# ConvFFN weight sums: base transfers issued by GpSimd, history copies on ScalarE, raw weight buffers parted

## The chip, the cores and the metric

One NeuronCore of a Trainium2 chip runs the whole program in one launch. The metric is device time in microseconds (us) for one execution; the median of a few runs is given. The engines are TensorE (PE, with its weight loads shown as PEld), VectorE (DVE), ScalarE (ACT), GpSimd (POOL) and SyncE (SP). SP only issues DMAs here. POOL issues DMAs too, and it does a few small copies.

## The reference, cut to what matters

The model is a two-layer decoder trunk in fp32. Layer 0 has a convolution and window-attention mixer, layer 1 a Mamba-2 mixer, and each layer ends with a gated feed-forward block with a short causal convolution. The change touches only these two blocks:

```python
def conv_ffn(h, hist, w_gate, w_up, conv_w, conv_b, w_down):
    gate = h @ w_gate
    padded = jnp.concatenate([hist, gate], axis=1)
    gc = causal_dwconv(padded, conv_w, conv_b)            # width 3
    y = (jax.nn.silu(gc) * (h @ w_up)) @ w_down
    return y, padded[:, -(FFN_CONV_WIDTH - 1):]
```

It runs on 512 prompt tokens (history zero) and 8 samples of 8 tokens, each with its own history of 2 gate rows. All 576 tokens sit side by side in the free dimension. D_MODEL is 1024, D_FF is 2816, which is 22 tiles of 128 channels.

## The kernel before, in words

**Numbers.** Every fp32 operand of a matmul is split into a rounded high part (`AF.Copy` on ACT, type fp32r) and a remainder (subtraction on DVE), and a product is three matmuls: high by high, high by low, low by high. The helper `split` of the class `Strassen` does this for weights at L83 (ACT) and L84 (DVE).

**Pairs.** After the first four gate tiles and two up tiles, the gate and up projections are computed for two output tiles at a time, by seven block products instead of eight (a Winograd form of Strassen's scheme). One such pair is a `Strassen` object around a `Gate` or `Up` job, and 19 pairs run in each feed-forward block. The activations' sums and differences (`hq`: B11, B21, T1 to T4, B22) are made once per block. The weights' sums are made per pair, and by DMA: `load` (from L62) brings the upper rows of both tiles into a raw buffer (`self.up`, 1024 columns). It also fills four tiles `st0` to `st3` of 512 columns: each gets a base from HBM by a plain DMA of SP (L69), and then a second DMA, issued by POOL, adds to it while it writes (L70, `accum_op=ADD`). The chain of a pair is s1 = A22 + A21, then s2 = A11 + s1, then s4 = A12 + s2; s3 = A11 + A21 stands alone. A last load (`self.low`, into a second raw buffer) brings A22 by itself; `sums` splits it into `dh` and `dl`.

**Where the splits go.** `alpha` splits the raw upper rows (products p1, p2), `beta` splits s1 and s2 (p5, p6), `gamma` splits s4 and s3 (p3, p7, run in the next pair's turn), and `dh`, `dl` serve p4. When a product is done, `c11`, `c12`, `c22`, `c21` of the job combine it into a gate buffer or into the up product.

**Gate buffers.** `gate_open` takes a buffer `gbuf` of 594 columns, clears its first two columns and copies the samples' histories into it (L572, L573, both POOL). `gate_done` copies the new histories out (L580, L581, POOL), runs the convolution over it (L584 on ACT, L586 twice on DVE) and the SiLU (L589, L590 on ACT).

**Down projection between the pairs.** When four gate-up products are complete, `down` or `down7` makes the work of their part of the down projection as a generator, and the loop over pairs advances it by one step after most products (`some(1)`). `down7` is again a seven-product form; its weights come as raw tiles `[128,1024]`, and its sums are made on DVE (L830 to L836). It asks for the tile after next at the end of `sums(m)`.

**Buffers and order.** Raw weights of all kinds (`weights_load`, L283) use one tag `wr` with three buffers. The tiles `st`, `gbuf`, `gconv` and many others come from one list of 67 slots (`S`, `free`): a new tile takes the slot that was given back longest ago, and its first write waits until the former tile's last reader is done. The program is written in one order in Python; a planner then fixes the order of each engine's instructions from its own estimate of durations, and within an engine and its queue that order is kept. So an instruction that waits on SP, POOL, ACT or DVE holds all that stands behind it there.

Of the kernel before, what the change touches and what calls it, by code (L numbers as in the profile page):

```python
# [8 lines left out]
F32 = mybir.dt.float32  # L9
F32R = mybir.dt.float32r  # L10
AF = mybir.ActivationFunctionType
# [3 lines left out]
P = 128  # L15
# [37 lines left out]
class Strassen:  # L53
# [3 lines left out]
    def __init__(self, b, job, n):  # L57
        self.b, self.nc, self.job = b, b.nc, job
        s = b.sr
        self.r, self.e, self.a = s[0][:, HALF[0]], s[1][:, HALF[0]], s[1][:, HALF[1]]  # L60

    def load(self):  # L62
        b = self.b
        up, low = self.job.src
        self.up = b.weights_load(up, 1024)
        s1, s2, s3, s4 = self.s = [b.S(f"st{i}", 512) for i in range(4)]
        for s, first, more in ((s1, low[:, 512:1024], low[:, 0:512]), (s2, up[:, 0:512], s1), (s4, up[:, 512:1024], s2),
                               (s3, up[:, 0:512], low[:, 0:512])):
            self.nc.sync.dma_start(s, first)  # L69
            self.nc.gpsimd.dma_start(s, more, accum_op=ADD)  # L70
        self.low = b.weights_load(low[:, 512:1024], 512)
        self.alpha()

    def sums(self, between=None):
        b = self.b
        if between:
            between()
        self.d = b.S("dh", 512, F32R), b.S("dl", 512, F32R)
        self.split(self.low[:, 0:512], *self.d)

    def split(self, src, hi, lo):
        nc = self.nc
# [76 lines left out]
class Builder:  # L159
# [3 lines left out]
    def __init__(self, nc, tc, d, stack):  # L163
        self.nc, self.tc, self.d = nc, tc, d
        self.const = stack.enter_context(tc.tile_pool(name="const", bufs=1))
        self.xp = stack.enter_context(tc.tile_pool(name="xp", bufs=1))
        self.wp = stack.enter_context(tc.tile_pool(name="wp", bufs=1))
        self.sp = stack.enter_context(tc.tile_pool(name="sp", bufs=1))
        self.pp = stack.enter_context(tc.tile_pool(name="pp", bufs=1, space=bass.MemoryType.PSUM))
        self.dp = stack.enter_context(tc.tile_pool(name="dp", bufs=1, space=bass.MemoryType.DRAM))  # L170
        self.rings = {"mm": [0, 1, 2, 3], "aux": [4, 5, 6, 7]}
        self.idle = list(range(self.NSLOT))
        self.used = {}
        self.small = None
        self.held = {}
# [103 lines left out]
        self.warm = self.const.tile([P, 1], F32, name="warm")  # L279
        nc.scalar.activation(self.warm, self.eps, AF.Sqrt)  # L280

    def weights_load(self, src, n):
        raw = self.wp.tile([P, 1024], F32, tag="wr", bufs=3, name="wr")  # L283
        srcs = src if isinstance(src, list) else [src]
        for i, s in enumerate(srcs):
            self.nc.sync.dma_start(raw[:, i * n // len(srcs):(i + 1) * n // len(srcs)], s)
        return raw
# [271 lines left out]
    def ffn(self, l, next_norm):  # L559
        nc, d = self.nc, self.d  # L560
        self.rings = {"mm": [0, 1, 2, 3, 4, 5], "aux": [6, 7]}
        hist = so = self.S("fhist", NF * 16)
        nc.sync.dma_start(hist, d["ffn_hist"][l])
        po = self.Z("fpo", NF * 2, bufs=1)
# [3 lines left out]
        samples = lambda g: g[:, 514:594].rearrange("p (b c) -> p b c", c=10)  # L568

        def gate_open(f):  # L570
            g = gbuf[f] = self.S("gbuf", 594)
            nc.gpsimd.memset(g[:, 0:2], 0.0)  # L572
            nc.gpsimd.tensor_copy(samples(g)[:, :, 0:2], hist[:, f * 16:f * 16 + 16].rearrange("p (b c) -> p b c", c=2))  # L573
            return g

        def gate_done(f):

            g = gbuf.pop(f)
            gs = samples(g)
            nc.gpsimd.tensor_copy(so[:, f * 16:f * 16 + 16].rearrange("p (b c) -> p b c", c=2), gs[:, :, 8:10])  # L580
            nc.gpsimd.tensor_copy(po[:, f * 2:f * 2 + 2], g[:, 512:514])  # L581
            cv = self.S("gconv", 594)
            w = lambda k: self.pv(f"fw{l}", f * 3 + k)
            nc.scalar.activation(cv[:, :592], g[:, 0:592], AF.Copy, scale=w(0))  # L584
            for k in (1, 2):
                nc.vector.scalar_tensor_tensor(cv[:, :592], g[:, k:592 + k], w(k), cv[:, :592], op0=MUL, op1=ADD)  # L586
            sl = sl_of[f] = self.S("gsilu")
            b = self.pv(f"fb{l}", f)
            nc.scalar.activation(sl[:, :NP], cv[:, :NP], AF.Silu, bias=b)  # L589
            nc.scalar.activation(bt(sl[:, NP:]), cv[:, 514:594].rearrange("p (b c) -> p b c", c=10)[:, :, 0:8],  # L590
                                 AF.Silu, bias=b)
            self.free(g, cv)
# [28 lines left out]
        def waiting(p):  # L621
            a, b = PARTS[p]
            if p - 1 in SEVEN:
                for f in range(a, (a + b) // 2):
                    operands(p, f)
            return a, b

        def lead_gate(f, later=False):
            def go(half, p):
                if half == 0:  # L630
                    nc.scalar.activation(gate_open(f)[:, 2:290], p[:, :HB], AF.Copy)
                    return
                g = gbuf[f]
                nc.scalar.activation(g[:, 290:514], p[:, 0:224], AF.Copy)
                nc.scalar.activation(samples(g)[:, :, 2:10], bt(p[:, 224:288]), AF.Copy)
                if not later:
                    gate_done(f)
            return go
# [29 lines left out]
        class Gate:  # L668
# [3 lines left out]
            def c11(me, u, v):  # L672
                nc.vector.tensor_tensor(gate_open(me.f)[:, 2:290], u, v, op=ADD)
# [7 lines left out]
            def c22(me, u, v):  # L681
                g = gate_open(me.f + 1)
                nc.vector.scalar_tensor_tensor(g[:, 290:514], u[:, 0:224], -1.0, v[:, 0:224], op0=MUL, op1=SUB)
                nc.vector.scalar_tensor_tensor(samples(g)[:, :, 2:10], bt(u[:, 224:HB]), -1.0, bt(v[:, 224:HB]), op0=MUL, op1=SUB)
# [42 lines left out]
        lead(0, g23, other)  # L727
        sums = self.combine()
        next(sums)
        lead(1, g01)  # L730
        u0 = [(self.whole(d["w_up"][l, 0]), lead_up(0))]
        next(sums)
        lead(1, g23[:1])
        u1 = [(self.whole(d["w_up"][l, 1]), lead_up(1))]
# [44 lines left out]
        def down7(p):  # L779
# [47 lines left out]
            def sums(m):  # L827
                a11, a12, a21, a22 = [raw[m][:, i * n:i * n + n] for i in range(4)]
                s12, s43 = s[m, 2], s[m, 3] = self.S("sd", 2 * n), self.S("sd", 2 * n)
                nc.vector.tensor_tensor(s12[:, 0:n], a21, a22, op=ADD)  # L830
                nc.vector.tensor_tensor(s12[:, n:2 * n], s12[:, 0:n], a11, op=ADD)
                nc.vector.tensor_tensor(s43[:, n:2 * n], a11, a21, op=ADD)
                nc.vector.tensor_tensor(s43[:, 0:n], a12, s12[:, n:2 * n], op=ADD)
                d = last[m] = self.S("dd", 2 * n, F32R)
                nc.scalar.activation(d[:, 0:n], a22, AF.Copy)
                nc.vector.tensor_tensor(d[:, n:2 * n], a22, d[:, 0:n].bitcast(F32), op=SUB)  # L836
                load(m + 2)

            def fourth(m):
# [3 lines left out]
                self.free(d)  # L843

            load(0)
            split(0, 1)
            quarters_of("T1")

            def go():
                sums(0)  # L850
                yield
                quarters_of("B22")
# [43 lines left out]
            todo += [Gate(f), Up(f - 2)]  # L896
        todo.append(Up(NF - 2))
        self.sr = [self.S("st"), self.S("st")]
        tiles = iter(())
        ready = 0  # L900

        def some(n):
            for _ in range(n):
                next(tiles, None)

        prev = None
        for n, job in enumerate(todo + [None]):
# [38 lines left out]
                ready += 1  # L946
            prev = new
        some(16)
        nc.sync.dma_start(d["ffn_s"][l], so)
        nc.sync.dma_start(d["ffn_p"][l], po)  # L950
        self.free(hist, self.sr, list(self.hq.values()))
# [2 lines left out]
        a, b = waiting(len(PARTS) - 1)  # L954
# [479 lines left out]
    def mix1(self):  # L1434
# [146 lines left out]
        def ssd(g):  # L1581
# [208 lines left out]
            for t in range(4):  # L1790
                if t == 0:
                    load(0)
                if t == 0:
                    ea2 = carried(0, False)
                pair = []
                for hh in range(2):
                    pair.append(decays(2 * t + hh))
                    yield
                last = outputs(t, ea2, pair)
                if t < 3:  # L1800
                    ea2 = carried(t + 1)
                if t == 2:
                    self.free(H)
                    H.clear()
                yield
                if t % 2:
                    turn(t // 2)
                    yield from finish(t // 2, last)
                    if t == 1:
                        load(1)  # L1810
                else:
                    begin(t // 2)
# [280 lines left out]
```

## Time and profile before

| | |
|---|---|
| median of 3 runs | 1507.55 us (1506.25 to 1511.75) |
| profiled execution, device time | 1503.02 us |
| its span, first to last instruction | 1501.2 us |
| PE, DVE, ACT, POOL busy | 1450.3, 1220.6, 856.4, 319.0 us |
| DMA, SP's queue (q1) | 185.87 MB |
| DMA, POOL's queue (q0) | 39.86 MB |

The profiled execution is one of the fast ones: its device time lies 4.5 us below the median of the three. A row of the waits has the engine, the tile and line that waited, what ended the wait, the total in us, the number of times and the longest. A row of the timeline has start, duration, engine, line, operation, tiles, and in brackets the idle time of the engine before it. The first feed-forward block's pairs run from about 262 to 560 us of the span, the second's from about 1085 to 1440 us.

### The profile page before, as it was taken

The page shows a single profiled execution, that of the slowest core. Times are in us where ns is not written, and L with a number is a line of the kernel's source. Part 1 is how long each engine was busy: PE and PEld are TensorE (multiplying, and loading weights), DVE is VectorE, ACT ScalarE, POOL GpSimd, SP SyncE. Part 2 cuts the span into 40 slices and gives each one's busy share as a digit, 9 for nine tenths or more (in the row PEclk, how much of TensorE's full clock was granted, in tenths as well). Part 3 has the DMA queues.
Part 4 walks back from the last instruction along what each step waited for, and adds up shares of the span by engine and source line. Part 5 has one row for each costly group of instructions (what it writes and reads, how often), then busy time and mean ns, then how long its engine had stood idle before and what let it go on. Part 6 is the DMA issues. An engine that isn't in the chain of part 4 may idle for free. (4 is left out here: it accounts for less than half of the span.)

```text
span 1501.2 us, 29480 instructions
## 1 busy us (share of the span) xinstructions
PE 1450.3 (97%) x11035; PEld 1376.0 (92%) x11035; DVE 1220.6 (81%) x2445; ACT 856.4 (57%) x1771; POOL 319.0 (21%) x517
## 2 busy tenths in 40 slices
PE   8999999999999989999999999999999999999999
PEld 7967799998999989998998997998999999999999
DVE  7968899698888856779798778677998889898673
ACT  6357467564655533487784664566457656464450
POOL 0026202322323220011203202112022232232210
PEclk9999999999999999999999999999999999999999
DMA  7504634867787773136245245245367877777831
GB/s 224 163 29 117 176 103 120 214 173 174 184 201 198 175 185 97 57 106 187 93 141 159 97 128 172 86 130 165 121 172 186 218 179 193 182 188 198 200 108 63
DMA packets 120925, 227.60 MB, mean 152 GB/s; under 512 B 25534, under 2 KB 32702, under 8 KB 120782
## 3 DMA queue, kind: packets, MB, share of 16 engines
q1 hardware_dynamic: 98894, 185.87, 38.9%
q0 software_dynamic: 21888, 39.86, 16.1%
q8 instruction: 86, 1.41, 0.4%
q14 instruction: 57, 0.47, 0.1%
HBM read 190.54 MB, written 15.21 MB: 137 GB/s over the span
## 5 line engine op out<-in xcount | busy, mean ns | idle before, releaser
L326 PE MATMUL mm<-hh,wh 128*128 128x288 f32 x864 | 262.5, 305 | 6.6 <-ACT wh L297 5.5
L329 PE MATMUL mm<-hl,wh 128*128 128x288 f32 x864 | 259.3, 301 | 0.3 <-DVE hl L968 0.2
L330 PE MATMUL mm<-hh,wl 128*128 128x288 f32 x864 | 258.4, 300 | 0.7 <-DVE wl L298 0.7
L326 PEld LDWEIGHTS mm<-hh,wh 128*128 128x128 f32 x864 | 164.4, 191 | 15.0 <-ACT wh L297 5.7
L330 PEld LDWEIGHTS mm<-hh,wl 128*128 128x128 f32 x864 | 164.2, 190 | 4.0 <-issue 1.8
L329 PEld LDWEIGHTS mm<-hl,wh 128*128 128x128 f32 x864 | 164.1, 190 | 3.4 <-issue 1.4
L297 ACT ACTIVATE wh<-wr 128x1024 fp32r<-128x1024 f32 (+1 forms) x97 | 101.6, 1048 | 99.7 <-PE mm L329 67.5
L298 DVE TENSOR_TENSOR wl<-wr,wh 128x1024 fp32r<-128x1024 f32 (+1 forms) x97 | 121.0, 1251 | 32.8 <-ACT wh L297 32.2
L83 ACT ACTIVATE wh<-st 128x512 fp32r<-128x512 f32 x152 | 91.0, 623 | 61.8 <-DMA st<-st 21.2
L70 POOL DMA_DIRECT2D st<-st x76 | 66.8, 885 | 272.1 <-DMA st<-st 53.3
L510 DVE TENSOR_TENSOR x<-x,mm 128x288 f32<-128x288 f32 x192 | 85.1, 449 | 43.4 <-PE mm L330 42.7
L326 PE MATMUL mm<-yh,wh 128*128 128x288 f32 x384 | 115.3, 301 | 0.2 <-DVE x L510 0.2
L330 PE MATMUL mm<-yh,wl 128*128 128x288 f32 x384 | 114.7, 299 | 0.0
L329 PE MATMUL mm<-yl,wh 128*128 128x288 f32 x384 | 114.1, 298 | 0.0
L84 DVE TENSOR_TENSOR wl<-st,wh 128x512 fp32r<-128x512 f32 x152 | 101.4, 684 | 13.0 <-ACT wh L83 12.9
L114 PE MATMUL x<-hqT,wh 128*128 128x288 f32 x304 | 90.6, 298 | 0.0
L117 PE MATMUL x<-hqT,wh 128*128 128x288 f32 x304 | 90.4, 297 | 0.0
L118 PE MATMUL x<-hqT,wl 128*128 128x288 f32 x304 | 90.1, 296 | 0.0
L586 DVE SCALAR_TENSOR_TENSOR gconv<-gbuf,par,gconv 128x592 f32<-128x592 f32 x88 | 72.9, 830 | 9.1 <-ACT gconv L584 8.4
L326 PEld LDWEIGHTS mm<-yh,wh 128*128 128x128 f32 x384 | 72.3, 188 | 3.5 <-issue 1.8
L330 PEld LDWEIGHTS mm<-yh,wl 128*128 128x128 f32 x384 | 72.3, 188 | 1.0 <-issue 0.4
L329 PEld LDWEIGHTS mm<-yl,wh 128*128 128x128 f32 x384 | 72.3, 188 | 0.5 <-issue 0.2
(462 smaller groups left out, 4830.3 us busy)
## 6 DMA issues: line engine op xcount, KB each, us to landing
st<-in_w_up SPq DMA_DIRECT2D x80, 256.0 KB, 5.1
wr<-in_w_down SPq DMA_DIRECT2D x80, 256.0 KB, 3.3
wr<-in_w_in_o SPq DMA_DIRECT2D x40, 512.0 KB, 3.6
st<-st POOLq DMA_DIRECT2D x76, 256.0 KB, 4.4
st<-in_w_gate SPq DMA_DIRECT2D x72, 256.0 KB, 3.1
wr<-in_w_gate SPq DMA_DIRECT2D x26, 512.0 KB, 4.1
wr<-in_w_up SPq DMA_DIRECT2D x24, 512.0 KB, 5.0
st<-in_w_up POOLq DMA_DIRECT2D x40, 256.0 KB, 5.8
```

The source lines that it names most:

```text
L83: nc.scalar.activation(hi, src, AF.Copy)
L84: nc.vector.tensor_tensor(lo, src, hi.bitcast(F32), op=SUB)
L114: m = nc.tensor.matmul(out, hi[:, ws], xh, start=first and k == 0, stop=False, skip_group_check=skip)
L117: nc.tensor.matmul(out, hi[:, ws], xl, start=False, stop=False, skip_group_check=skip)
L118: nc.tensor.matmul(out, lo[:, ws], xh, start=False, stop=k == 3, skip_group_check=skip)
L297: nc.scalar.activation(hi[:, a:b], raw[:, a:b], AF.Copy)
L298: nc.vector.tensor_tensor(lo[:, a:b], raw[:, a:b], hi[:, a:b].bitcast(F32), op=SUB)
L326: first = nc.tensor.matmul(out, hi[:, ws], xh[:, sl], start=i == 0, stop=False)
L329: nc.tensor.matmul(out, hi[:, ws], xl[:, sl], start=False, stop=False)
L330: nc.tensor.matmul(out, lo[:, ws], xh[:, sl], start=False, stop=i == n - 1)
L510: nc.vector.tensor_tensor(self.x[m][:, sl], self.x[m][:, sl], p[:, :HB], op=ADD)
L586: nc.vector.scalar_tensor_tensor(cv[:, :592], g[:, k:592 + k], w(k), cv[:, :592], op0=MUL, op1=ADD)
```

## The change

- The bases of the four sums are issued by POOL (`nc.gpsimd.dma_start`) in the order s1, s3, s2, s4, all four ahead of the four accumulating DMAs, which now come in the same order. SP no longer issues them.
- `self.low` leaves the raw buffers: it goes into a slot of the list `S` (tile `a22`), which is given back once it is split.
- The clearing of two columns in `gate_open` goes from POOL to DVE; the copies of the histories in `gate_open` and `gate_done` go from POOL to ACT (three per gate tile).
- The tag `wr` with three buffers becomes three tags with one buffer each, handed out in rotation. While the pairs run, two of them serve only the pairs' upper rows and the third serves only the down weights; elsewhere all three rotate as before.

```diff
     def load(self):
         b = self.b
         up, low = self.job.src
-        self.up = b.weights_load(up, 1024)
+        self.up = b.weights_load(up, 1024, b.ring_up)
         s1, s2, s3, s4 = self.s = [b.S(f"st{i}", 512) for i in range(4)]
-        for s, first, more in ((s1, low[:, 512:1024], low[:, 0:512]), (s2, up[:, 0:512], s1), (s4, up[:, 512:1024], s2),
-                               (s3, up[:, 0:512], low[:, 0:512])):
-            self.nc.sync.dma_start(s, first)
+        for s, first in ((s1, low[:, 512:1024]), (s3, up[:, 0:512]), (s2, up[:, 0:512]), (s4, up[:, 512:1024])):
+            self.nc.gpsimd.dma_start(s, first)
+        for s, more in ((s1, low[:, 0:512]), (s3, low[:, 0:512]), (s2, s1), (s4, s2)):
             self.nc.gpsimd.dma_start(s, more, accum_op=ADD)
-        self.low = b.weights_load(low[:, 512:1024], 512)
+        self.low = b.S("a22", 512)
+        self.nc.sync.dma_start(self.low, low[:, 512:1024])
         self.alpha()
...
-        self.split(self.low[:, 0:512], *self.d)
+        self.split(self.low, *self.d)
+        b.free(self.low)
...
+        self.ring_wr = [0, 1, 2]
...
-    def weights_load(self, src, n):
-        raw = self.wp.tile([P, 1024], F32, tag="wr", bufs=3, name="wr")
+    def weights_load(self, src, n, ring=None):
+        ring = ring or self.ring_wr
+        ring.append(ring.pop(0))
+        raw = self.wp.tile([P, 1024], F32, tag=f"wr{ring[-1]}", bufs=1, name="wr")
...
             g = gbuf[f] = self.S("gbuf", 594)
-            nc.gpsimd.memset(g[:, 0:2], 0.0)
-            nc.gpsimd.tensor_copy(samples(g)[:, :, 0:2], hist[:, f * 16:f * 16 + 16].rearrange("p (b c) -> p b c", c=2))
+            nc.vector.memset(g[:, 0:2], 0.0)
+            nc.scalar.activation(samples(g)[:, :, 0:2], hist[:, f * 16:f * 16 + 16].rearrange("p (b c) -> p b c", c=2), AF.Copy)
...
-            nc.gpsimd.tensor_copy(so[:, f * 16:f * 16 + 16].rearrange("p (b c) -> p b c", c=2), gs[:, :, 8:10])
-            nc.gpsimd.tensor_copy(po[:, f * 2:f * 2 + 2], g[:, 512:514])
+            nc.scalar.activation(so[:, f * 16:f * 16 + 16].rearrange("p (b c) -> p b c", c=2), gs[:, :, 8:10], AF.Copy)
+            nc.scalar.activation(po[:, f * 2:f * 2 + 2], g[:, 512:514], AF.Copy)
...
+        self.ring_up, self.ring_wr = self.ring_wr[:2], self.ring_wr[2:]
         tiles = iter(())
...
         some(16)
+        self.ring_wr = self.ring_up + self.ring_wr
```

## The prediction

> **What bounds the kernel now.** I read the page first: PE is busy 97% of the span, so only PE's idle time is to be had. The change acts between 262 and 560 us and between 1085 and 1440 us (the pairs of the two feed-forward blocks), so I took the busy times of these two stretches. The columns are the stretch, its length, busy time and count for PE, PEld, DVE, ACT and POOL, the granted clock, the DMA share and GB/s.
>
> ```profile
> PE 1450.3 (97%) x11035; PEld 1376.0 (92%) x11035; DVE 1220.6 (81%) x2445; ACT 856.4 (57%) x1771; POOL 319.0 (21%) x517
> ```
>
> ```profile
> 262.00:560.00 298.00, 279.54 (x2056) 277.28 (x2055) 243.51 (x516) 160.28 (x317) 81.96 (x131) 0.98 0.75 188
> 1085.00:1440.00 355.00, 343.47 (x2562) 339.99 (x2561) 304.85 (x646) 204.97 (x413) 96.92 (x156) 1.00 0.74 189
> ```
>
> PE idles 18.5 us in the first stretch and 11.5 us in the second: 30.0 us is all that the change can win there. PE's waits by releaser, first block and then second:
>
> ```profile
> PE dy L773 <- DVE x L818: 7.9, 3, 3.6
> PE y L114 <- DVE gbuf L678: 5.5, 1, 5.5
> PE dx L773 <- DVE x L818: 2.2, 3, 1.1
> PE z L114 <- DVE x L510: 1.7, 1, 1.7
> PE x L114 <- DVE gbuf L684: 1.2, 1, 1.2
> ```
>
> ```profile
> PE dx L773 <- DVE x L818: 5.4, 5, 1.7
> PE dy L773 <- DVE x L818: 3.4, 2, 2.0
> PE z L114 <- DVE x L510: 2.1, 2, 1.5
> PE x L114 <- DVE gbuf L684: 0.4, 1, 0.4
> ```
>
> PE always waits for a late DVE. DVE is late because ACT, which splits the weights first, stood waiting for a DMA. The lines of the code with what waited for them say so (L286 loads raw weights, L70 accumulates):
>
> ```profile
>   ACT dh L83: 61.8, 23
> ```
>
> ```profile
>   POOL st L70: 81.3, 25
>   ACT wh L83: 36.8, 12
> ```
>
> Three kinds can be told apart in the timelines. **A:** the raw `low` lands late, ACT sits at `dh`, and all behind it slips:
>
> ```profile
> 1410.56 0.63 ACT L83 ACTIVATE dh<-wr 128x512 fp32r<-128x512 f32 x1 [3.69 <-DMA wr<-in_w_up]
> 1411.80 0.76 DVE L349 TENSOR_TENSOR yl<-gsilu,yh 128x576 fp32r<-128x576 f32 x1 [3.70 <-ACT yh L348]
> 1413.71 0.40 PE L773 MATMUL dx<-yT,dd 128*128 128x288 f32 x1 [1.57 <-DVE x L818]
> ```
>
> **B:** at the end of the first block SP stands from 529.4 to 535.3 before a down weight that has no raw buffer; two bases come only behind it, and their sums end 17 us later:
>
> ```profile
> 529.02 0.33 SPq L69 DMA_DIRECT2D st<-in_w_up  x1
> 535.29 0.82 SPq L286 DMA_DIRECT2D wr<-in_w_down  x2
> 536.20 0.41 SPq L69 DMA_DIRECT2D st<-in_w_up  x1
> 553.08 0.63 ACT L83 ACTIVATE wh<-st 128x512 fp32r<-128x512 f32 x1 [6.94 <-DMA st<-st]
> 555.01 0.58 PE L114 MATMUL y<-hqT,wh 128*128 128x288 f32 x1 [5.48 <-DVE gbuf L678]
> ```
>
> **C:** beside the down parts (the waits on `dy`) a base waits for its slot, given back by the convolution of the gate tile before; then come its landing, the accumulation, ACT and DVE:
>
> ```profile
> 402.45 0.83 DVE L586 SCALAR_TENSOR_TENSOR gconv<-gbuf,par,gconv 128x592 f32<-128x592 f32 x1
> 403.43 0.33 SPq L69 DMA_DIRECT2D st<-in_w_gate  x1
> 407.37 0.89 POOL L70 DMA_DIRECT2D st<-st  x1 [3.62 <-DMA st<-in_w_gate]
> 412.48 0.63 ACT L83 ACTIVATE wh<-st 128x512 fp32r<-128x512 f32 x1 [2.13 <-DMA st<-st]
> 414.78 0.37 PE L773 MATMUL dy<-yq,vh 128*128 128x288 f32 x1 [2.05 <-DVE x L818]
> ```
>
> **The change part by part.** Durations of what moves (minimum, median, maximum in ns for the issues and copies; a landing row belongs to the line above it: L70, L69, then L286, the raw loads; last come the two shapes nearest to the new operations):
>
> ```profile
> L70 POOL DMA_DIRECT2D st<-st x76: 860/870/1369, 178.8 to 1427.7; - x76
> DMA to landing us min/median/max: 3.2/4.9/8.6
> L69 SPq DMA_DIRECT2D st<-in_w_up x80: 327/370/1147, 168.5 to 1415.8; - x80
> L69 SPq DMA_DIRECT2D st<-in_w_gate x72: 327/328/463, 166.7 to 1389.7; - x72
> DMA to landing us min/median/max: 2.6/4.1/7.3
> L286 SPq DMA_DIRECT2D wr<-in_w_down x96: 327/404/703, 245.5 to 1457.5; - x96
> DMA to landing us min/median/max: 2.0/3.6/9.6
> L573 POOL COPY gbuf<-fhist x44: 191/558/4585, 166.9 to 1410.9; 128x16 f32<-128x16 f32 x44
> L635 ACT ACTIVATE gbuf<-mm 128x64 f32<-128x64 f32 x8 | 1.7, 215 | 0.0
> L1503 DVE MEMSET sp_v<- 128x32 f32 x1 | 0.1, 85 | 0.0
> ```
>
> *Load of `low` (A).* It no longer needs a raw buffer, and four DMAs leave SP's queue around it. The two accumulations from `st` per pair, 76 in all, make 38 pairs; 23 waits at `dh` are three pairs in five. The waits on dx, z and x sum to 2.2+1.7+1.2+5.4+2.1+0.4 = 13.0 us; three fifths are 7.9 us. I take 6 of it, since a slot given back late can still hold the load. Bounds: 0 (slots hold it as the buffer did) and -13.0.
>
> *Bases off SP and down weights in their own buffer (B).* The bases no longer stand behind a raw buffer's wait. Of 5.5 us I take 5, since the chain of three landings stays. Bounds 0 and -5.5.
>
> *Bases on POOL (C).* The 152 bases cost POOL 870 instead of SP's 327 to 370 ns. That is 132 us of issuing more; POOL loses 44 memsets and 132 copies. It is busy 82.0+96.9 of 653 us, so its idle time hides it. On the five waits on `dy` the base is on the path: +0.54 us each. The two copies that `gate_done` now puts on ACT ahead of the convolution delay the slot: 2 x 0.215 = +0.43 each. That is 5 x 0.97 = +4.9 us, the upper end. The lower end is -11.3 (7.9+3.4, all of it gone, if queues and not slots were what held these bases). I take +2: the row of L586 ends at 403.28, just ahead of the base's issue, so slots hold them, but earlier `low` and freed queues give some of it back.
>
> *Memset on DVE, copies on ACT.* 44 x 0.085 = 3.7 us on DVE, which is busy 548.4 of 653 us, so at most 3.1 on the path; it stands right ahead of the addition into the same tile, so its wait for the slot is not new. 132 x 0.215 = 28 us on ACT, busy 365.3 of 653 us; what lies ahead of the convolution is counted above, the copy in `gate_open` hides in ACT's idle time. POOL's copies, up to 4.6 us long, leave the way of the accumulations. I take +0.5, bounds 0 and +3.1. If ACT's cover were gone, the rest would cost 44 x 0.215 = 9.5 us.
>
> *One raw buffer for down weights.* SP then waits until `sums` and the split of one tile are done before it loads the next, and `low` and the upper rows queue behind it. Today's waits of this kind on SP:
>
> ```profile
> SPq L286 <- DVE dd L836: 42.9, 10, 8.0
> ```
>
> The next tile is asked for two steps of the down work before it is split, a step being about a quarter of a pair, 17.2/4 us (653 us over 38 pairs), so 8.6 us against the raw loads' median landing of 3.6: I take +0.5. Bounds 0 and +24: with the row's longest landing, 9.6, and 0.33 for the first of its two issues each tile is 1.3 us late, and 18 tiles are loaded so (three in each of six `down7` parts).
>
> The Trainium skill's page "SBUF — State Buffer" (section "SBUF: two separate sides") warns of just this move: descriptors of DMAs issued from GpSimd are written by GpSimd and starve while DVE holds the port pair that they share, and it advises issuing from SP. The trace does not bear it out for these shapes: L70's issues take 860 at least and 870 in the median with DVE 84% busy. If the 1369 of the row's maximum held for the five bases on the path, the sum would be 2.5 us worse.
>
> **Sum:** -6 -5 +2 +0.5 +0.5 = -8 us. The profiled execution took 1503.0 us; on its own time that gives 1495. Against the median of the runs, 4.5 us higher, it gives 1507.55 - 8 = **1499.5 us**.
>
> **Rivals.** *R1, the queues were the cause of everything:* A, B and C all fall away but for a third: -2/3 of 30.0 = -20, 1487.5 us. For it: POOL's 25 and ACT's 35 waits above are all for DMAs. Against: the slot rows of C.
>
> *R2, no change:* the loads wait for slots where they waited for buffers and SP, or the DMA engines are the limit (0.75 busy in both stretches, and the bytes stay). Then only the small costs stay: about 1508 us. The skill's page "DMA: Bandwidth & Descriptors" ("Issuing engines are not separate DMA queues") leans this way: all issuers share the same 16 engines.
>
> *R3, slower:* POOL becomes the one queue in which bases and accumulations hold each other up. In program order a pair's s4 accumulation can be issued only after three landings: base s1, sum s1, sum s2. With the row's 4.9 each and 0.87 to issue the last, that is 15.6 us, under the 17.2 of a pair. It decides where landings pass (17.2-0.87)/3 = 5.4 us, since then the next pair's bases, queued behind, come late. At 6.4, between median and maximum, it costs 3 us a pair. Slots are short beside the `down7` parts, 24 pairs; one in three of them makes 8 x 3 = +24, and A's -6 stays: +18, 1525.5 us. For it: landings reach 8.6. Against: the planner can put the next pair's bases ahead of the waiting accumulation.
>
> **How the numbers follow.** Forecast 0.40 (its own range -15 to -2), R1 0.18, R2 0.12, R3 0.30. No change means within 0.5%, 7.5 us, about what a measurement here can tell. Faster: 0.6 of the forecast's 0.40 plus R1, 0.42. Same: the rest of the forecast and R2, 0.28. Slower: R3, 0.30. The range leaves a tenth at each end: below, R1 with a little more, 1484; above, R3 to just short of its price and of the bounds' sum, 1524.
>
> **What would show it.** Right: waits of ACT at `dh` fall from 61.8 to under 30 us; the 5.5 us before y near 555 goes; the waits on `dy` stay at 8 to 14 us; PE's idle time in the two stretches falls from 30 to about 22. Wrong: POOL waits for `st` landings grow well past the 81.3 us and bases are issued after them (R3); ACT waits at `dh` for a22 as long as before (R2); the waits on `dy` vanish (R1).

## The result and the profile after

The changed kernel takes **1553.17 us** (median of 4 runs, 1547.49 to 1556.14); the kernel before takes 1509.65 beside it (4 runs, 1506.25 to 1515.99). The ratio is **1.028, 95% interval 1.023 to 1.033**: 2.8% slower, where 1499.5 us and a range up to 1524 were forecast. The profiled execution took 1547.49 us, with a span of 1545.7 against 1501.2 before.

The page of the changed kernel, busy times:

```profile
PE 1462.6 (95%) x11035; PEld 1383.4 (89%) x11035; DVE 1222.0 (79%) x2489; ACT 868.9 (56%) x1902; POOL 341.8 (22%) x493
```

PE does the same 11035 matmuls, and DVE's busy time has hardly changed (1220.6 before). Where the 44.5 us went is seen by stage. I cut the span at the first and last pair product of each feed-forward block (rows 1 and 3 are the pairs, row 2 lies between the two blocks; what is ahead of the first pair and behind the last is the same within 0.5 us), in the columns of the prediction's table. The kernel before:

```profile
255.90:588.60 332.70, 314.24 (x2317) 311.98 (x2316) 271.45 (x567) 178.62 (x350) 83.82 (x134) 0.98 0.72 184
588.60:1139.30 550.70, 543.09 (x4168) 504.32 (x4167) 446.51 (x806) 346.46 (x738) 94.17 (x164) 1.00 0.42 128
1139.30:1462.50 323.20, 311.76 (x2318) 309.10 (x2317) 271.46 (x566) 179.68 (x350) 84.24 (x134) 0.99 0.73 186
```

The changed kernel:

```profile
256.30:604.40 348.10, 317.38 (x2318) 313.97 (x2317) 271.15 (x581) 182.65 (x400) 96.84 (x136) 0.97 0.69 173
604.40:1164.40 560.00, 547.45 (x4169) 504.93 (x4168) 447.20 (x814) 349.03 (x755) 92.58 (x153) 0.99 0.41 127
1164.40:1507.00 342.60, 317.41 (x2317) 314.84 (x2316) 271.05 (x579) 182.99 (x398) 96.33 (x134) 0.97 0.68 173
```

The pairs lose 15.4 + 19.4 = 34.8 us: PE's idle time there grows from 29.9 to 55.9 us (length less busy time, both stretches), and its busy time by 8.8 us for the same matmuls, at a lower granted clock. The stretch between the blocks, which the change was not thought to touch, loses 9.3 us. The DMA engines are no busier than before (share 0.72 and 0.73 before, 0.69 and 0.68 now), so they did not become the limit.

Waits of PE, ACT and POOL in the changed kernel, by releaser (total, times, longest); they answer to the rows on `dy`, `y`, `z` and `wh` of the prediction:

```profile
PE dy L778 <- DVE x L823: 13.9, 7, 5.3
PE y L116 <- DVE gbuf L683: 9.8, 1, 9.8
PE dy L778 <- ACT gsilu L595: 9.2, 3, 4.8
PE z L116 <- DVE x L515: 6.6, 1, 6.6
...
ACT wh L85 <- DMA st<-st: 53.1, 14, 16.4
```

The kernel before: what waited for the bases (L69; us, times), and the same wait of ACT:

```profile
  POOL st L70: 79.6, 26
```

```profile
ACT wh L83 <- DMA st<-st: 21.2, 8, 6.9
```

The groups of the bases (L68), then of the accumulations (L70), then of the load of `low` (L72), in the changed kernel, each with what waited for it:

```profile
L68 POOL DMA_DIRECT2D st<-in_w_up x80: 536/830/1180, 174.4 to 1460.5; - x80
L68 POOL DMA_DIRECT2D st<-in_w_gate x72: 536/581/1147, 167.7 to 1429.3; - x72
...
  POOL st L70: 194.9, 62
...
DMA to landing us min/median/max: 2.8/4.9/8.5
...
L70 POOL DMA_DIRECT2D st<-st x76: 847/882/1213, 177.9 to 1470.4; - x76
...
  POOL st L70: 123.6, 45
  ACT wh L85: 73.7, 18
...
DMA to landing us min/median/max: 3.2/4.5/8.7
...
  ACT dh L85: 32.7, 14
```

POOL now stands before accumulations 194.9 us (62 times) until a **base** has landed; before it was 79.6 us (26 times). Its waits for the landing of another sum, the prediction's 81.3 us (25 times), are now 123.6 (45 times). (The rows of waits by tile cannot tell a base from s1 and s3, whose accumulations read HBM too; the rows by line can.) ACT waits 53.1 us for the finished sums, before 21.2. A base lands in 4.9 us in the median (4.1 when SP issued it), an accumulation in 4.5 (4.9 before). So POOL's waits for bases became more frequent and not longer: 79.6/26 and 194.9/62 are both 3.1 us. The same place as B in the prediction shows how the queue works now. Timeline of the changed kernel at the end of the first block, POOL's transfers with the ACT and PE instructions that waited for them:

```profile
544.15 0.90 POOL L68 DMA_DIRECT2D st<-in_w_up  x1
550.17 0.86 POOL L70 DMA_DIRECT2D st<-in_w_up  x1 [5.11 <-DMA st<-in_w_up]
550.74 0.87 POOL L68 DMA_DIRECT2D st<-in_w_up  x1
557.10 0.87 POOL L70 DMA_DIRECT2D st<-st  x1 [5.49 <-DMA st<-in_w_up]
557.68 1.94 POOL L68 DMA_DIRECT2D st<-in_w_up  x3
562.90 0.92 POOL L70 DMA_DIRECT2D st<-in_w_up  x1 [3.28 <-DMA st<-in_w_up]
...
568.32 0.63 ACT L85 ACTIVATE wh<-st 128x512 fp32r<-128x512 f32 x1 [16.44 <-DMA st<-st]
...
570.84 0.58 PE L116 MATMUL y<-hqT,wh 128*128 128x288 f32 x1 [9.85 <-DVE gbuf L683]
```

A base (544.15), then an accumulation that waits 5.11 us for it, and only then the next base (550.74), whose own accumulation waits 5.49 us, and only then three more bases. No base can go out from POOL while it stands there; when SP issued the bases, that wait of POOL did not hold them. The wait before `y`, 5.5 us in the prediction's B, was to go; it became 9.85 us.

### The profile page after: what moved, and what is told of

The parts are those of the page before. It is cut to its first block, busy times and chain, and to the rows that moved or that the text cites. A ratio compares the mean times of both kernels' runs of the same rounds, so it can differ in the third digit from the quotient of the medians.

```text
span 1545.7 us, 29262 instructions
## 1 busy us (share of the span) xinstructions
PE 1462.6 (95%) x11035; PEld 1383.4 (89%) x11035; DVE 1222.0 (79%) x2489; ACT 868.9 (56%) x1902; POOL 341.8 (22%) x493
## 3 DMA queue, kind: packets, MB, share of 16 engines
q1 hardware_dynamic: 77006, 146.01, 29.9%
## 5 line engine op out<-in xcount | busy, mean ns | idle before, releaser
L85 ACT ACTIVATE wh<-st 128x512 fp32r<-128x512 f32 x152 | 91.5, 623 | 96.9 <-DMA st<-st 53.1
L70 POOL DMA_DIRECT2D st<-st x76 | 67.5, 893 | 228.5 <-DMA st<-st 67.4
L68 POOL DMA_DIRECT2D st<-in_w_gate x72 | 48.3, 683 | 178.7 <-DVE wl L86 82.1
L1765 POOL TENSOR_TENSOR h<-h,small 128x512 f32<-128x512 f32 x32 | 43.0, 1374 | 137.7 <-PE pyo L1759 137.7
```

The costliest lines, as they stand in the source:

```text
L85: nc.scalar.activation(hi, src, AF.Copy)
```

## The experiments

The expectations name theories by letters, and where a letter comes back with another meaning, the expectation says which: Q is one in-order POOL queue, B the raw buffers, C the copies, O the order of the bases, R the rotation. All ratios are to the kernel before, measured beside each kernel on the same chip. For the overview I add from the traces the length of the two stretches of pairs together, that of the stretch between the blocks (both cut as above), and POOL's waits for a base's landing (the row of POOL among those who waited for the line of the bases, as shown above).

| kernel | ratio, 95% interval | pairs us | between us | POOL waits for bases, us (times) |
|---|---|---|---|---|
| before | 1 | 655.9 | 550.7 | 79.6 (26) |
| changed | 1.028, 1.023 to 1.033 | 690.7 | 560.0 | 194.9 (62) |
| bases_only | 1.029, 1.025 to 1.033 | 700.8 | 551.3 | 192.0 (67) |
| bases_paired | 1.026, 1.021 to 1.031 | 696.3 | 551.7 | 211.4 (75) |
| s1_pool | 1.022, 1.017 to 1.028 | 695.7 | 550.5 | 172.9 (46) |
| bases_flat | 1.032, 1.028 to 1.035 | 707.8 | 550.0 | 280.7 (93) |
| bases_ring | 1.026, 1.022 to 1.029 | 700.8 | 548.9 | 195.3 (68) |
| flat_sp | 1.005, 1.002 to 1.007 | 670.2 | 549.9 | 119.3 (40) |
| order_only | 1.003, 1.000 to 1.005 | 668.8 | 550.6 | 53.3 (18) |
| pool_extra | 1.005, 1.002 to 1.007 | 667.9 | 550.3 | 67.4 (23) |
| copies_only | 1.002, 0.998 to 1.005 | 661.0 | 549.4 | 75.4 (17) |
| low_only | 1.007, 1.004 to 1.011 | 658.6 | 554.2 | 57.2 (15) |
| rot_only | 1.011, 1.007 to 1.015 | 676.1 | 557.1 | 70.1 (22) |
| rot_skip | 1.011, 1.006 to 1.015 | 668.8 | 557.1 | 77.8 (21) |
| buffers_only | 1.017, 1.014 to 1.020 | 671.5 | 559.0 | 76.2 (22) |
| all_but_bases | 1.018, 1.015 to 1.022 | 666.1 | 560.6 | 84.0 (16) |

The stretches are those of one profiled execution, the ratios those of several runs, so the two need not agree to a few us (order_only's stretches are 13 us longer, its ratio gives 4; low_only was profiled at 1508.97 us, the shortest of its ten runs, whose median is 1523.66).

### The parts of the change

**bases_only**, the kernel before with only the bases moved:

```diff
-        for s, first, more in ((s1, ...), (s2, ...), (s4, ...), (s3, ...)):
-            self.nc.sync.dma_start(s, first)
+        for s, first in ((s1, low[:, 512:1024]), (s3, up[:, 0:512]), (s2, up[:, 0:512]), (s4, up[:, 512:1024])):
+            self.nc.gpsimd.dma_start(s, first)
+        for s, more in ((s1, low[:, 0:512]), (s3, low[:, 0:512]), (s2, s1), (s4, s2)):
             self.nc.gpsimd.dma_start(s, more, accum_op=ADD)
```

> The kernel before with the bases of the four sums issued by POOL (order s1, s3, s2, s4, all ahead of the accumulating DMAs), nothing else changed. Theory Q (one queue: a base that waits for its slot holds the accumulations behind it on POOL, an accumulation that waits for a landing holds the bases of the next pair): 25 to 45 us slower than before, PE's waits on dy, y, z well above the 30.0 us of before, waits of ACT at the split of st from 36.8 to over 60 us. Theory B (the raw buffers are the cause: fixed rotation, and one buffer for down weights): within 8 us of before. Theory C (the copies on ACT and the memset on DVE are the cause): within 8 us of before.

**buffers_only**, the kernel before with `low` in a slot, the three tags in rotation and their parting while the pairs run:

```diff
-        self.low = b.weights_load(low[:, 512:1024], 512)
+        self.low = b.S("a22", 512)
+        self.nc.sync.dma_start(self.low, low[:, 512:1024])
...
-        raw = self.wp.tile([P, 1024], F32, tag="wr", bufs=3, name="wr")
+        ring = ring or self.ring_wr
+        ring.append(ring.pop(0))
+        raw = self.wp.tile([P, 1024], F32, tag=f"wr{ring[-1]}", bufs=1, name="wr")
...
+        self.ring_up, self.ring_wr = self.ring_wr[:2], self.ring_wr[2:]
```

> The kernel before with low in a slot of the list and the raw buffers handed out in rotation and parted, bases still on SP, copies still on POOL. Theory Q: 5 to 15 us faster, since ACT's 61.8 us of waiting at dh fall by half and nothing else gets worse. Theory B: 15 to 40 us slower, about 9 of it in the stretch between the two blocks' pairs (550.7 us before, 560.0 after). Theory C: within 8 us of before.

**copies_only**, the kernel before with the clearing on DVE and the copies on ACT:

```diff
-            nc.gpsimd.memset(g[:, 0:2], 0.0)
-            nc.gpsimd.tensor_copy(samples(g)[:, :, 0:2], hist...)
+            nc.vector.memset(g[:, 0:2], 0.0)
+            nc.scalar.activation(samples(g)[:, :, 0:2], hist..., AF.Copy)
...
-            nc.gpsimd.tensor_copy(...)
-            nc.gpsimd.tensor_copy(...)
+            nc.scalar.activation(..., AF.Copy)
+            nc.scalar.activation(..., AF.Copy)
```

> The kernel before with the clearing of gbuf on DVE and the copies of histories on ACT, nothing else. Theory Q and theory B: within 8 us of before. Theory C (copies wait on ACT in order for gbuf and hold the splits behind them, and put 0.4 us ahead of each convolution): 10 to 30 us slower.

**all_but_bases**, the changed kernel with the bases back on SP in the old order:

```diff
-            self.nc.gpsimd.dma_start(s, first)
+            self.nc.sync.dma_start(s, first)
```

> The changed kernel with the bases back on SP in the order and place of before (each ahead of its accumulation). Theory Q: 1490 to 1505 us, the gain that was forecast for the load of low; PE idle in the pairs under 30 us. Theory B and theory C: still 1530 us or more.

Measured: bases_only 1.029, buffers_only 1.017, copies_only 1.002, all_but_bases 1.018. The bases alone give the whole loss of the change, and all of it in the pairs (655.9 to 700.8 us; between the blocks 551.3). The buffers alone lose 1.7%, a third of it outside the pairs (8.3 of 24.6 us). The copies cost nothing that can be measured. buffers_only and all_but_bases (1527.55 us) went as theory B had it, or nearly so (15 to 40 us slower; 1530 us or more), and not as Q had it (5 to 15 us faster; 1490 to 1505 us): the bases are the larger loss, but not the only one. The two losses do not add up: 2.9 and 1.7% apart, 2.8% together, so once the bases are on POOL, the other buffers cost no more, and giving the bases back to SP in the changed kernel wins only a third of the loss.

### What the bases cost on POOL

**bases_paired** puts each base right ahead of its own accumulation, and **order_only** keeps SP but issues all four bases first, in the new order:

```diff
 bases_paired
-            self.nc.sync.dma_start(s, first)
+            self.nc.gpsimd.dma_start(s, first)
 order_only
+        for s, first in ((s1, ...), (s3, ...), (s2, ...), (s4, ...)):
+            self.nc.sync.dma_start(s, first)
+        for s, more in ((s1, low[:, 0:512]), (s3, low[:, 0:512]), (s2, s1), (s4, s2)):
+            self.nc.gpsimd.dma_start(s, more, accum_op=ADD)
```

> The kernel before with the bases issued by POOL, each right ahead of its own accumulation in the order of before (s1, s2, s4, s3). Theory Q (one queue holds both kinds, whatever the order): 25 to 60 us slower, like bases_only (42.7 slower). Theory O (what hurts is that all four bases stand ahead of all four accumulations, with s3 ahead of s2): under 15 us slower.

> The kernel before with all four bases ahead of the four accumulations, in the order s1, s3, s2, s4, but the bases still on SP. Theory Q: within 8 us of before. Theory O: 15 us slower or more, as bases_only.

Measured: 1.026 and 1.003. The order within the pair explains neither: on POOL both orders lose, on SP the new order loses a quarter of a per cent.

**s1_pool** moves one base of the four; **bases_flat** moves all, but no accumulation reads another sum, so the chain of landings is gone; **flat_sp** is its companion with SP's bases. Both leave out the chained sums, so s2 and s4 are not what the products need, and only their time is of use:

```diff
 s1_pool
-            self.nc.sync.dma_start(s, first)
+            (self.nc.gpsimd if s is s1 else self.nc.sync).dma_start(s, first)
 bases_flat, against bases_only
-        for s, more in ((s1, low[:, 0:512]), (s3, low[:, 0:512]), (s2, s1), (s4, s2)):
+        for s, more in ((s1, low[:, 0:512]), (s3, low[:, 0:512]), (s2, low[:, 0:512]), (s4, low[:, 0:512])):
 flat_sp, against the kernel before
-        for s, first, more in ((s1, ...), (s2, up[:, 0:512], s1), (s4, up[:, 512:1024], s2), (s3, ...)):
+        for s, first, more in ((s1, ...), (s2, up[:, 0:512], low[:, 0:512]), (s4, up[:, 512:1024], low[:, 0:512]), (s3, ...)):
```

> The kernel before, with only the base of s1 issued by GpSimd, right ahead of its accumulation; the other three bases stay with SP. Theory Q (one in-order queue: a base that stands on GpSimd cannot be issued before the accumulations of the pair before are through, so its landing is waited out there): one base a pair is enough, since s1 heads the chain s1, s2, s4; GpSimd then waits one landing of about 4.7 us a pair where it waited none, and the ratio is 1.012 to 1.028, far over a quarter of what four bases cost. Rival N (each DMA put on GpSimd costs its share: 0.87 us of issuing, one more entry in the queue): a quarter of the 2.9% of four bases, 1.007, at most 1.010.

> All bases on GpSimd, four ahead of the four accumulations, but every accumulation adds rows from HBM (the lower left block) and none reads another sum; so s2 and s4 are not the sums of the reference, and the chain of three landings is gone (about one landing is left a pair). To be held against the same kernel with SP's bases. Theory Q: GpSimd is blocked per pair for one landing and eight issues, about 4.7+8x0.85 = 11.5 us, under the 17.2 us of a pair, so it catches up and bases go out ahead: at most 1.010 above the kernel with SP's bases. Rival P (plain transfers from GpSimd are themselves slow or late, whatever waits there): the same 2.6 to 2.9% above it.

> The companion: bases issued by SP as before, every accumulation adds the same rows from HBM and none reads another sum (s2 and s4 are not the sums of the reference). It shows what the chain of sums costs the kernel before. If the chain of landings holds up sums there too (the waits on y and dy of the profile before): 0.990 to 0.997. If DVE's and ACT's order sets those waits: 0.997 to 1.002.

Measured: 1.022, 1.032 and 1.005. One base alone costs most of what four cost: not a price per transfer, so N falls. But bases_flat lies 2.7% above its companion where my theory said at most 1.0%: **the chain of three landings is not what costs**, and that part of theory Q fell. The 2.7% is what the rival P of that run named, that plain transfers from GpSimd are late in themselves. flat_sp, too, lies above both ranges named for it (1.002 at most): without the chain the kernel with SP's bases is no faster. What waited for the bases' line in s1_pool (all four bases), then bases_flat, then flat_sp:

```profile
  POOL st L70: 172.9, 46
```

```profile
  POOL st L70: 280.7, 93
```

```profile
  POOL st L70: 119.3, 40
```

With a base on POOL, the accumulations stand 173 to 281 us waiting for bases, whether sums hang on each other or not; with SP's bases 53 to 119 (the table).

That left as rivals, beside transfers that land late in themselves, GpSimd's issuing and the room for its descriptors. **pool_extra** adds four small plain transfers per pair that wait for nothing; **bases_ring** doubles the room:

```diff
 pool_extra
             self.nc.sync.dma_start(s, first)
+            k, b.extra_n = b.extra_n, b.extra_n + 1
+            b.tc.keep_in_program_order(self.nc.gpsimd.dma_start(b.extra[:, k:k + 1], first[:, 0:1]))
             self.nc.gpsimd.dma_start(s, more, accum_op=ADD)
 bases_ring, against bases_only
-    nc = bacc.Bacc("TRN2", ..., dynamic_dma_scratch_size=1024)
+    nc = bacc.Bacc("TRN2", ..., dynamic_dma_scratch_size=2048)
```

> The kernel before with SP's bases, and four more plain transfers of GpSimd per pair (one column of 128 rows each, into a tile that nothing reads, 152 in all, none of them waiting for a slot or a landing). They cost GpSimd the issues of the bases without their waits. Theory Q (what costs is that a base stands in one in-order queue behind accumulations that wait for landings): the ratio is at most 1.004. Rival P (GpSimd's own issuing is the cost: 0.54 to 0.87 us each in its instruction stream and its queue, ahead of the accumulations): 1.02 or more, as with the bases.

> The bases on GpSimd as in the run with the bases alone, with twice the room for the descriptors that GpSimd writes for its queue. Theory Q: waits for landings and slots do not depend on that room, 1.025 to 1.032 as with the bases alone. Rival D (GpSimd's queue is short of descriptor room once it carries twice as many transfers, so issues wait for earlier transfers to finish): 1.012 or less.

Measured: 1.005 and 1.026. The first block's pairs by engine, first in pool_extra and then in bases_only (the fifth engine column is POOL):

```profile
255.70:591.90 336.20, 317.76 (x2317) 315.29 (x2316) 272.61 (x567) 178.15 (x350) 125.22 (x201) 0.97 0.73 182
```

```profile
255.90:602.60 346.70, 317.49 (x2317) 314.90 (x2316) 272.69 (x567) 178.67 (x350) 118.66 (x200) 0.97 0.69 176
```

POOL is as busy with transfers that nobody waits for, 125.2 against 118.7 us, and the kernel loses half a per cent instead of nearly three; more room changes nothing. So it is neither the issuing nor the room. The transfers of pool_extra are of one column each, so they do not test whether the moving of a whole base is late from POOL. The landings speak against that: a base lands 0.8 us later from POOL (4.9 against 4.1 us), part of which is the longer issue. In s1_pool 38 bases are moved; if each of them made PE late by all of it, that would be 38 x 0.8 = 30 us, and s1_pool loses 34.6 (1540.75 less 1506.16).

What is left is the **waits in one in-order queue**: an accumulation stands there until its base has landed and holds back the bases behind it, as in the timeline, and a base that waits for its slot stands in the way of accumulations. With SP's bases the two kinds of waits ran beside each other. All six kernels with a base on POOL lose 2.2 to 3.2%, in either order and with or without the chain. No run isolates the wait itself, though, by moving the bases to a third engine or ahead of the waiting accumulations. The half per cent of pool_extra (a little over the 1.004 that Q allowed) bounds the price of the issues.

### What the buffers cost

**low_only** is the kernel before with only `low` in a slot (one tag, three buffers); **rot_only** only hands out three tags in rotation, without parting (both edits are shown above).

> The kernel before with low in a slot of the list instead of a raw buffer; the other raw weights keep one tag with three buffers. Theory of the prediction (term A, the late low is three fifths of the waits on dx, z and x): 3 to 12 us faster, waits at dh under 35 us instead of 61.8. Rival (the slot comes back as late as the buffer did, and the list is shorter by one): waits at dh still 50 us or more, time within 5 us of before or slower.

> The kernel before with the one tag of three raw buffers made into three tags handed out in rotation, all three for everything; low stays in a raw buffer, nothing parted. Theory R (the fixed rotation alone costs the part that lies between the blocks' pairs): 6 to 12 us slower, the stretch between the pairs 557 to 562 us instead of 550.7, the pairs themselves within 6 us of before. Theory P (the parting, one buffer for the down weights, is all of it): within 5 us of before.

Measured: 1.007 and 1.011. Neither is a gain. `low` in a slot does not come earlier: ACT's waits at `dh` for its load are 58.9 us (19 times) in low_only, against the 61.8 (23 times) of before, as the rival in its expectation had it:

```profile
ACT dh L85 <- DMA a<-in_w_up: 37.9, 12, 5.6
...
ACT dh L85 <- DMA a<-in_w_gate: 21.0, 7, 8.3
```

PE's waits move from `dy` to `dx`; its largest wait in low_only (`dx` was 7.7 us in 8 waits over the whole span before):

```profile
PE dx L775 <- DVE x L820: 19.4, 10, 3.8
```

Rotation without any parting costs 1.1%, about 16 us, where 6 to 12 were expected. In the profiled execution 6.4 us of its loss lie between the blocks, as expected, and 20.2 in the pairs, which were to stay within 6; the runs do not take the part in the pairs further apart. Between the blocks every kernel with rotation loses (557 to 561 us against 549 to 554). The first suspect there was the last down weight of the block. SP's raw loads in rot_only at the block's end:

```profile
582.30 3.00 SPq L289 DMA_DIRECT2D wr<-in_w_down  x4
...
598.97 0.80 SPq L289 DMA_DIRECT2D wr<-in_w_down  x2
```

The last down weight waits for its own buffer until 598.97, 4.9 us after the last pair product (594.1). In the kernel before all six issues of the three last tiles were out by 584.42, 4.2 us ahead of the last pair product (588.6):

```profile
576.83 7.59 SPq L286 DMA_DIRECT2D wr<-in_w_down  x6
```

**rot_skip** lets the four down weights at the block's end pass over the buffer that is held longest:

```diff
+            held = self.skip.pop() if self.skip else None
-            ring.append(ring.pop(0))
+            ring.append(ring.pop(1 if ring[0] == held else 0))
...
+        self.skip = [self.ring_wr[-1]] * 4
         self.out_proj(...)
```

> Three raw buffers in fixed rotation as in the change, but the last four down weights of each block pass over the one buffer that the part before them holds longest (its tile is split in two halves, the second late). Theory H (a load in rotation waits for its own buffer while another is free: with rotation alone the last down weight was issued at 599.0 us, behind the split of that second half, 5 us after the pairs' end; in the kernel before at 583.6, 5 us ahead of it): the stretch between the blocks' pairs falls from 557.1 to 553 us or less (550.7 before), the ratio from 1.0105 to 1.005 or a little less. Rival G (the plan as a whole is another one, the place is chance): the stretch stays at 556 to 558 us and the ratio at 1.009 to 1.012.

Measured: 1.011, and the stretch stays at 557.1 us. The same three tiles now leave between 581.61 and 591.05, ahead of the last pair product (593.4):

```profile
581.61 9.44 SPq L291 DMA_DIRECT2D wr<-in_w_down  x6
```

Nothing is won by it, so theory H falls, and its rival G had both numbers. Where the time between the blocks goes can be seen, though. Two windows, 20 to 50 and 50 to 100 us after the last pair product, in the kernel before, then in rot_only, then in rot_skip:

```profile
608.60:638.60 30.00, 28.90 (x230) 26.95 (x229) 24.98 (x57) 14.14 (x33) 1.81 (x13) 1.00 0.21 69
638.60:688.60 50.00, 50.00 (x378) 47.25 (x377) 39.16 (x73) 42.15 (x86) 5.79 (x12) 1.00 0.42 121
```

```profile
614.10:644.10 30.00, 27.68 (x212) 24.82 (x211) 24.47 (x57) 13.98 (x33) 1.55 (x13) 1.00 0.15 50
644.10:694.10 50.00, 47.78 (x350) 44.06 (x350) 34.90 (x65) 38.47 (x76) 5.22 (x12) 1.00 0.42 125
```

```profile
613.40:643.40 30.00, 27.69 (x212) 24.78 (x210) 24.45 (x58) 13.98 (x33) 1.56 (x13) 1.00 0.15 49
643.40:693.40 50.00, 47.96 (x351) 44.28 (x351) 34.77 (x65) 39.06 (x79) 5.76 (x12) 1.00 0.41 126
```

With rotation PE has done 46 matmuls fewer at that point (608 less 562); at 50.00/378 = 0.132 us each that is 6.1 of the 6.4 us. So the loss between the blocks lies at the end of the block and the start of the layer 1 mixer. Which load or split there causes it is open; only the last down weight is ruled out.

## Why the prediction was wrong, step by step

**What bounds the kernel** was right: PE's lateness behind DVE, ACT and DMA in the pairs is where time is won and lost. Wrong was that only the pairs can change: 9.3 of the 44.5 us arose between the blocks.

**A, load of `low` (-6).** The sign by which it was to be known nearly came: waits at `dh` fell from 61.8 to 32.7 us in the changed kernel, where under 30 was named. But the load out of the raw buffer did not do it, and the gain did not come. low_only, this edit alone, is 0.7% slower, and its waits at `dh` stay at 58.9 us. The step that failed is "it no longer needs a raw buffer", taken as an earlier landing; what came is the lower bound of the term, "slots hold it as the buffer did", and the sign that the prediction gave to R2. The waits fell only where the bases had left SP as well; whether `low` came earlier there or ACT came later to `dh`, from its waits for sums, was not told apart.

**B, bases off SP (-5).** Failed. The bases do not stand behind SP's wait for a raw buffer any more; they stand behind POOL's wait for a landing, and 5.5 us became 9.85.

**C, bases on POOL (+2).** This is the term that decides, and it was mis-sized: alone it is 1.029, about 43 us on 1507.55 us, where the upper end of the bounds was +4.9. The issues were timed rightly or even too high (medians 581 and 830 ns; 870 was taken), and their price, by pool_extra, is about half a per cent (0.2 to 0.7). The step of the prediction that failed is "busy 82.0+96.9 of 653 us, so its idle time hides it". POOL's idle time was no room: POOL spends much of it standing before an accumulation, 194.9 us for bases and 123.6 for sums. And only the five waits on `dy` were charged, though the accumulations of every pair pass through that queue.

**Memset and copies (+0.5), down weights in one raw buffer (+0.5).** The first is not contradicted: copies_only 1.002, interval 0.998 to 1.005. The second was sized as waits of SP within the pairs. There is such a wait, ACT's before the raw down weights, in the changed kernel and then before:

```profile
ACT dd L840 <- DMA wr<-in_w_down: 18.4, 8, 3.7
```

```profile
ACT dd L835 <- DMA wr<-in_w_down: 4.4, 1, 4.4
```

The 14 us more are inside its bounds of 0 to 24, but the one buffer is not their cause: rot_only, where the down weights use all three, has 24.1 us (7 times) of the same wait. And rotation by itself, which the working never priced, costs 1.1%. The parting adds nothing that the runs can tell from the sum of the two single edits: 1.011 with rotation, 1.007 with `low`, 1.017 with both and the parting.

**The rivals.** R3 named the mechanism that came, with a chance of 0.30 and 1525.5 us; it is 1553. Its price was built on a wrong condition, a chain of three landings that has to pass the 17.2 us of a pair. By the changed kernel's rows the chain is 4.9 + 4.5 + 4.5 + 0.87 = 14.8 us, below it, and bases_flat, which has no such chain, loses as much. By these runs it needs no overflow: the loss comes with a chain below the pair's length, and without a chain. R3's own counterargument, that the planner can put the next pair's bases ahead of a waiting accumulation, did not hold at the place that the timeline shows: there the base of 550.74 stands behind the accumulation of 550.17. And "A's -6 stays" was lost with A. R1 fell (the queue was moved, not removed), and so did R2 as a whole (the small costs were not all), though its reason, loads that wait for slots as they waited for buffers, is what low_only shows.

**The Trainium skill.** The page "SBUF — State Buffer" was right to advise SP for these transfers, but for another reason than it gives here: L70's issues from `st` take 882 ns in the median (870 before), 1213 at most (1369 before), with DVE 78% busy in the pairs, and their landings did not grow, so no starving shows. A sentence that bears on what happened is in "DMA: Bandwidth & Descriptors", section "Anatomy of one DMA — SWDGE (gpsimd) path": any wait for a semaphore is made by the issuing sequencer, ahead of the dispatch. The timeline above agrees: the accumulation holds POOL 5.11 and 5.49 us until its base has landed. By the section quoted in the prediction, "Issuing engines are not separate DMA queues", moving an issue should only save or cost issuing time; here it cost 2.9%, and the measurement decides: the waits of the two engines are separate, as the waits above show.

**What stays open:** why the losses of bases and buffers do not add up, what is late under rotation, in the pairs and between the blocks, and why one base costs nearly as much as four (POOL waits for bases nearly as long, 172.9 against 192.0 us; the trace does not tell why). No kernel tried beats the one before.

## What to carry to other kernels

An engine that is 25% busy may still have no room for a transfer: look at what stands at the head of its queue, and for how long, before moving anything behind it that others wait for. In this kernel the transfers that wait for a buffer and those that wait for data did better on different issuers, and moving even one across cost most of what moving all of them costs. A sign that comes true, like the shorter waits at `dh`, does not show that its cause is the one named: one run with that edit alone does. When one tag with several buffers becomes several tags in a fixed rotation, every user of those buffers is changed, also in parts of the program that the edit does not name; measure that step by itself.

## What the runs showed of the hardware

A stall costs more than its length. Three windows of the changed kernel: a stall of PE that ends at 417.42 (4.76 us), the 3.4 us behind it, and the next 3.4:

```profile
410.00:417.40 7.40, 1.85 (x12) 1.63 (x13) 5.66 (x12) 5.88 (x17) 4.25 (x7) 1.00 0.66 139
417.40:420.80 3.40, 3.38 (x15) 3.40 (x16) 3.13 (x9) 1.44 (x4) 2.08 (x4) 0.55 0.96 223
420.80:424.20 3.40, 3.40 (x27) 3.40 (x26) 3.28 (x9) 1.58 (x2) 0.00 (x0) 0.94 1.00 238
```

The granted clock falls to 0.55 right behind the stall, and PE does 15 matmuls where it does 27 in the next window: 12 matmuls, about 1.5 us, on top of the stall. More such stalls fit the growth of PE's busy time in the pairs by 8.8 us for the same work. The Trainium skill's page "TensorE: Matmul & The Clock Gate" (section "HAM oscillation — how this bites in real kernels") says that an idle gap of more than about 3.4 us returns the clock to half; this stall agrees. A shorter one did it here too. In the kernel before, behind the stall of 2.05 us that ends at 414.78 (C in the prediction), the clock is 0.75 over the first of these two windows, and PE does 22 matmuls where it does 28 in the next:

```profile
417.40:420.80 3.40, 3.40 (x22) 3.40 (x21) 3.19 (x8) 1.45 (x3) 0.88 (x1) 0.75 1.11 242
420.80:424.20 3.40, 3.40 (x28) 3.40 (x27) 2.11 (x6) 1.52 (x4) 0.88 (x1) 1.00 0.86 197
```

The prediction counted stalls at their length only.
